# The experts of a second half's last token block are chosen once row 72 of the block ahead of it is with the vector engine

## The chip, the cores and the metric

The kernel runs on one core of a Trainium2 chip. The metric is device time in microseconds (us) from launch to end. Five engines work side by side: TensorE (PE in the profile, its weight loads PEld), VectorE (DVE), ScalarE (ACT), GpSimd (POOL) and SyncE (SP). Each takes its instructions in the order in which they stand in its own list. SP does nothing here but start plain DMAs; POOL does little but start the gathers, which are DMAs whose source rows come from a list of indices.

## The reference, cut to what matters

Two layers of a decoder over 512 tokens of width 1024. A layer mixes tokens in three ways (a gated recurrence, attention, a state-space scan), projects, adds, and ends with a layer of experts:

```python
for l in range(2):
    u = rms_norm(x, ...) @ w_in[l]
    m = concat([hgrn2(u), dilated_attention(u), ssd(u)])
    h = x + m @ w_out[l]
    x = h + peer(rms_norm(h))
# peer, for each token: 8 heads; a head scores 2 x 128 sub-keys, keeps the best 16 of either
# half, and of their 256 sums the best 16: an expert is (i, j), one of 128 x 128
# gate = softmax over the 16; down, up: tables of 16384 rows of 1024
# y = sum over the 8 x 16 = 128 chosen experts of  up[e] * gate[e] * gelu(<down[e], h_norm>)
```

For each token 128 rows of `down` and 128 rows of `up` are wanted, at places that depend on the data.

## The kernel before

**Tiling.** The 512 tokens are four blocks of 128. A half h is two blocks, j = 0 and 1. So (l, h, j) names a block of a layer. A *row* is one of a block's 128 experts for all its 128 tokens: one gather of 128 x 1024 float32 (512 KB), and one VectorE instruction that uses it.

**The pieces.** The mixers of a half are m00, m01, m10, m11 (layer, half). `choose` picks the experts of a half in four groups, (j, g) = (0,0), (0,1), (1,0), (1,1): g is which four heads. A group is about a hundred short VectorE instructions with a few of ScalarE between them. It ends with a write of 64 columns of the block's index list, `idx`. With four groups in each of four halves there are sixteen choices, numbered here 0 to 15 in order: 4 to 7 are layer 0's second half, 12 to 15 layer 1's. `experts_down` (d010 is layer 0, half 1, block 0) gathers rows of `down`: rows 0 to 63 use the indices of group g = 0, rows 64 to 127 those of g = 1; VectorE then multiplies the row by the normed tokens and sums (`g<-g,xn`), into column i of `a`. `experts_up_rows` (u010, u011, u111) gathers rows of `up`, and VectorE adds them to the block (`xv<-g,c,xv`). `experts_up_dense` (u00 for the first half of layer 0, u10 for layer 1's and the third block) does the same sum without gathers: SP streams the whole table as 128-row tiles `u`, VectorE builds one-hot operands (`oj`, `oi`, `co`) from the indices, PE turns them into coefficients `ct` (the builds: `ps<-co,oj`) and multiplies `u` by these (the uses: `ps<-u,ct`). At its end VectorE adds PE's sums to the tokens (`ux<-ux,ps`).

**What sets the order.** Three queues of Python generators are interleaved by a virtual clock: fg (m00, m01, u00, m10, m11, u10), bg (all experts_down and experts_up_rows) and tk (choose). A generator that yields "?x" waits until another has yielded "x". `experts_down` yields "?t.." ahead of row 64, `choose` of a second half yields "?b.." ahead of its second group (the first build of the dense part has been written down). The stream is then put in the engines' lists by a list scheduler that works with its own estimate of times; `behind(a, b)` tells it that `a` has to come after `b` on their engine, without a semaphore. Here every first `max` of choices 5, 6, 7 (and 13, 14, 15) stands behind `lead[l][-1]`, the last `co` of the first build, and rows 0 to 31 of d010 and d110 behind the others of `lead[l]`, two rows to one `co`. Buffers: eight for gathered rows, seven for weights and `u` tiles.

**How the pieces meet.** u00 runs beside d010 and d011; its end (`ux`) lets m10 begin, beside which u010 and u011 run. m11 needs u011 and the tokens of the second half, and after it come layer 1's d110 and d111 beside u10, and u111. On VectorE all are in one list. The profile puts nearly all instructions on L1383, the line of the helper that records them; the gathers are on L1068.

Of the kernel before, what the change touches and what calls it, by code (L numbers as in the profile page):

```python
# [29 lines left out]
FIRST = 0  # L30
AHEAD = 2
BIAS_AT = 16
ROWS = ((0, 1), (1,))
PE_ROWS = ((0, 0), (0, 0))
D = 1024
# [80 lines left out]
def hybrid_kernel(ctx: ExitStack, tc: tile.TileContext, x, w, small, rows, keys_t, rel_bias,  # L116
# [23 lines left out]
    def scr(shape, tag, dt=F32, bufs=None, pool=None):  # L140
        cnt[0] += 1
        return (pool or scope[0]).tile(shape, dt, name=f"{tag}_{cnt[0]}", tag=tag, bufs=bufs or BUFS.get(tag))

    def keep(shape, tag, dt=F32, bufs=4):
        return scr(shape, tag, dt, bufs=bufs, pool=pp)
# [83 lines left out]
    lead = [[] for _ in range(L)]  # L229
# [730 lines left out]
    def choose(l, h):  # L960

        e = st[l, h]
        qp = e.pop("qp")
        scr = lambda shape, tag, dt=F32, bufs=2: keep(shape, "k" + tag, dt, bufs)
        for j, g in ((0, 0), (0, 1), (1, 0), (1, 1)):
            if h and (j, g) == (0, 1):
                yield f"?b{l}"
            if (j, g) == (0, 1):
                yield f"?m{l}{h}"
            if g == 0:  # L970
# [11 lines left out]
            for c in range(2):  # L982
                sb = scr([P, 4, P], "s2")
                S.activation(sb, pc[c], AF.Copy, scale=e["y"][j])
                for a in range(4):
                    o, oi, i = sv[:, c, a, :], si[:, c, a, :], sb[:, a, :]
                    r = V.max(o[:, 0:8], i)
                    if h and (j or g):
                        behind(r.ins, lead[l][-1])
                    elif not h and (j or g):  # L990
                        behind(r.ins, e["last"])
                    V.max_index(oi[:, 0:8], o[:, 0:8], i)
                    V.match_replace(i, o[:, 0:8], i, -3e38)
                    V.max(o[:, 8:16], i)
                    V.max_index(oi[:, 8:16], o[:, 8:16], i)
                    yield
# [19 lines left out]
            r = scr([P, 2, 64], "rk")  # L1016
# [30 lines left out]
            r = V.tensor_tensor(e["idx"][j][:, 64 * g:64 * g + 64], ij[:, 0], ij[:, 1], OP.add)  # L1047
# [12 lines left out]
    def behind(ins, lead):  # L1060

        tc.add_manual_dep(ins, lead.name,
                          mybir.DependencyInfo(mybir.DependencyClass.NoSync, mybir.DependencyReason.DATA),
                          reason="the leading work first")

    def gather(table, idx, i):
        t = gslot([P, D])
        nc.gpsimd.indirect_dma_start(out=t, out_offset=None, in_=table,  # L1068
                                     in_offset=bass.IndirectOffsetOnAxis(ap=idx[:, i:i + 1], axis=0))
        return t  # L1070


    def experts_down(l, h, j):
        d = st[l, h]
        a = scr([P, P], "a", pool=pp, bufs=1)
        for i in range(P):
            if i == 64:
                yield f"?t{l}{h}{j}1"
            t = gather(down, d["idx"][j], i)
            r = V.scalar_tensor_tensor(t, t, 1.0, d["xn"][j], op0=OP.mult, op1=OP.mult, accum_out=a[:, i:i + 1])  # L1080
            g = i // RPG
            if (h, j) == (1, 0) and g < len(lead[l]):
                behind(r.ins, lead[l][g])
            yield
        u = scr([P, P], "u", pool=pp, bufs=1)
        c = keep([P, P], "c")
        V.tensor_tensor(u, a, a, OP.mult)
        V.tensor_scalar(u, u, 0.044715, 1.0, op0=OP.mult, op1=OP.add)
        V.tensor_tensor(u, u, a, OP.mult)
        V.tensor_scalar(u, u, -2.0 * math.sqrt(2.0 / math.pi), 80.0, op0=OP.mult, op1=OP.min)  # L1090
        S.activation(u, u, AF.Exp)
        V.tensor_tensor(a, a, d["gate"][j].rearrange("p a b -> p (a b)"), OP.mult)
        V.tensor_scalar(u, u, 1.0, None, op0=OP.add)
        V.reciprocal(u, u)
        V.tensor_tensor(c, a, u, OP.mult)
        d.setdefault("c", []).append(c)
        yield
# [4 lines left out]
    def experts_up_rows(l, j, n_pe):  # L1102

        d = st[l, 1]
        xv = keep([P, D], "xv", bufs=1)
        nc.sync.dma_start(xv, xd[(2 + j) * P:(3 + j) * P, :])
        on_pe = [i for i in range(P) if spread(i, n_pe)]
        acc = [bank([P, 512]) for _ in range(2)] if on_pe else []
        for i in range(P):
            t = gather(up, d["idx"][j], i)  # L1110
            if i in on_pe:
                dg = keep([P, P], "dg", bufs=2)
                S.activation(dg, ident, AF.Copy, scale=d["c"][j][:, i:i + 1])
                for n in range(2):
                    PE.matmul(acc[n], dg, t[:, n * 512:(n + 1) * 512], start=(i == on_pe[0]), stop=(i == on_pe[-1]))
            else:
                V.scalar_tensor_tensor(xv, t, d["c"][j][:, i:i + 1], xv, op0=OP.mult, op1=OP.add)
            yield
        for n, p in enumerate(acc):
            o = xv[:, n * 512:(n + 1) * 512]  # L1120
            V.tensor_tensor(o, o, p, OP.add)
        nc.sync.dma_start(out_rows(l, 2 + j), xv)
        yield
# [161 lines left out]
    def first():  # L1285
        def later():
            for _ in range(BIAS_AT):
                yield
            yield from make_bias()
# [10 lines left out]
    for l in range(L):  # L1300
        for h in range(2):
            tk.append((f"k{l}{h}", lambda l=l, h=h: choose(l, h), [f"p{l}{h}"]))
            for j in range(2):
                bg.append((f"d{l}{h}{j}", lambda l=l, h=h, j=j: experts_down(l, h, j), [f"t{l}{h}{j}0"]))
        for j in ROWS[l]:
            bg.append((f"u{l}1{j}", lambda l=l, j=j: experts_up_rows(l, j, PE_ROWS[l][j]), []))
# [5 lines left out]
    while any(pos[k] < len(queues[k]) for k in range(NQ)):  # L1312
        ready = []
        for k in range(NQ):
            if pos[k] == len(queues[k]):
                continue
            if gen[k] is None:
                name, f, deps = queues[k][pos[k]]
# [29 lines left out]
        if k == 1:  # L1348
            f = fg[pos[0]][0] if pos[0] < len(fg) else ""
# [115 lines left out]
```

## Time and profile before

| | us |
|---|---|
| runs | 3186.52, 3188.92, 3195.61 |
| median | 3188.92 |
| the profiled execution, its own time | 3198.11 |
| its span | 3196.2 |
| busy: PE, VectorE, POOL, ScalarE | 2409.3, 2680.0, 1778.9, 645.2 |

The span is from the first to the last instruction, and 1.9 us of the execution lie outside it. Times below are us from the span's start. VectorE is the busiest engine (84%), DMA stands near its full share in most of the forty slices, and PE is full where the dense part runs. No one of them fills the span: which one holds it up changes from stage to stage, so it is read stage by stage.

### The profile page before, as it was taken

The numbers are of one execution on the slowest core, as the hardware profiler recorded it, in microseconds if no ns is written. First come the engines' busy times: TensorE is split into PE (matmuls) and PEld (weight loads), VectorE is DVE, ScalarE is ACT, GpSimd is POOL, SyncE is SP. The second block draws the span as 40 slices with busy tenths as digits, with TensorE's granted clock in tenths as the row PEclk, the third lists the DMA queues.
The fourth block names the chain that finished last, engine by engine and source line by source line (L and its number), as shares of the span: only waits on it lengthen the run. The fifth ranks groups of instructions, "written<-read, shape, count | busy, mean of one in ns | idle before, by whom it ended". The sixth has DMA issues, their size and how long they took to land.

```text
span 3196.2 us, 45630 instructions
## 1 busy us (share of the span) xinstructions
PE 2409.3 (75%) x16115; PEld 1485.9 (46%) x16115; DVE 2680.0 (84%) x6050; ACT 645.2 (20%) x2076; POOL 1778.9 (56%) x1425
## 2 busy tenths in 40 slices
PE   7888777512999999687760467773189999799878
PEld 6776554411555554465540345543145455444423
DVE  7669998799999886587889999978999988878852
ACT  4554331100110000234220144221111110101100
POOL 0006677477346565475657666775752665666530
PEclk9889876755999999898585688676589999899999
DMA  5439999988769999999899999898785999899998
GB/s 189 143 109 339 356 337 329 335 292 303 289 262 397 358 359 415 350 399 358 295 373 369 403 346 366 304 355 317 260 329 180 395 371 362 298 402 357 377 420 332
DMA packets 291745, 1049.27 MB, mean 328 GB/s; under 512 B 33040, under 2 KB 33936, under 8 KB 291516
## 3 DMA queue, kind: packets, MB, share of 16 engines
q0 software_dynamic: 203824, 740.27, 62.1%
q1 hardware_dynamic: 87692, 306.08, 25.5%
q8 instruction: 127, 2.08, 0.2%
q14 instruction: 102, 0.84, 0.1%
HBM read 1037.82 MB, written 10.37 MB: 328 GB/s over the span
## 4 chain that ended last, share of the span: by engine, by line
PE 34%; DVE 32%; issue 13%; DMA 12%; POOL 5%; ACT 3%; POOLq 0%; DVEq 0%; SPq 0%; ACTq 0%
PE ps L1383 34%; DVE g L1383 14%; DMA g<-in_down_dram,idx 7%; POOL g L1068 5%; DMA g<-in_up_dram,idx 5%; DVE ksi L1383 2%; DVE oj L1383 2%; DVE xv L1383 2%; DVE co L1383 2%; DVE ks L1383 2%; DVE keq L1383 2%; DVE ksv L1383 1%; ACT s L1383 1%; DVE s L1383 1%; DVE krk L1383 1%
## 5 line engine op out<-in xcount | busy, mean ns | idle before, releaser
L1068 POOL DMA_INDIRECT g<-in_down_dram,idx x1024 | 1323.4, 1292 | 849.9 <-DVE g L1383 281.0
L1383 DVE SCALAR_TENSOR_TENSOR g<-g,xn 128x1024 f32<-128x1024 f32 x1024 | 1226.5, 1218 | 120.8 <-DMA g<-in_down_dram,idx 118.5
L1383 PE MATMUL ps<-u,ct 128*128 128x512 f32 x2560 | 1157.1, 604 | 34.4 <-DMA u<-in_up_dram 33.6
L1383 PEld LDWEIGHTS ps<-u,ct 128*128 128x128 f32 x2560 | 475.5, 192 | 616.9 <-issue 531.7
L1068 POOL DMA_INDIRECT g<-in_up_dram,idx x384 | 447.4, 1165 | 286.2 <-DVE xv L1383 172.1
L1383 DVE SCALAR_TENSOR_TENSOR xv<-g,c,xv 128x1024 f32<-128x1024 f32 x384 | 492.2, 1282 | 97.3 <-DMA g<-in_up_dram,idx 84.1
L1383 PE MATMUL ps<-co,oj 128*128 128x32 bf16 (+1 forms) x7296 | 214.0, 180 | 238.1 <-DVE co L1383 237.1
L1383 PEld LDWEIGHTS <-oj 128*128 128x128 bf16 x7296 | 209.2, 98 | 308.8 <-DVE co L1383 173.5
L1383 ACT ACTIVATE ct<-ps 128x128 f32<-128x128 f32 (+1 forms) x704 | 128.7, 278 | 933.3 <-PE ps L1383 933.2
L1383 PE MATMUL ps<-ident,s 128*128 128x128 f32 (+1 forms) x276 | 67.7, 388 | 281.3 <-ACT s L1383 240.1
L1383 DVE TENSOR_TENSOR oj<-ijt,iota_j 128x2048 bf16<-128x2048 bf16 x152 | 184.2, 1216 | 58.4 <-PE ps L1383 58.4
L1383 PEld LDWEIGHTS ps<-ident,s 128*128 128x128 f32 (+1 forms) x276 | 45.4, 197 | 297.6 <-ACT s L1383 248.9
L1383 DVE TENSOR_TENSOR co<-oi,cp 128x768 bf16<-128x768 bf16 (+1 forms) x304 | 161.7, 569 | 12.3 <-PE ps L1383 12.2
L1383 ACT ACTIVATE s<-ps 128x512 f32<-128x512 f32 (+5 forms) x143 | 62.3, 439 | 166.4 <-PE ps L1383 151.4
L752 POOL MEMSET diag<- 128x256 f32 x4 | 1.3, 316 | 162.3 <-DVE ksv L1383 162.3
L1383 PE MATMUL ps<-g,g 128*128 128x256 f32 (+2 forms) x280 | 89.7, 321 | 1.5 <-DVE g L1383 1.5
L1383 PE MATMUL ps<-T,g 128*128 128x256 f32 x400 | 81.7, 301 | 3.1 <-ACT T L1383 3.1
L1383 DVE DVE_READ_ACCUMULATOR g<-g,xn 128x1 f32 x1024 | 80.6, 79 | 0.0
L1383 DVE MAX8 ksv<-ks 128x8 f32<-128x128 f32 x256 | 57.4, 277 | 22.5 <-ACT ks L1383 22.5
L1383 DVE TENSOR_TENSOR oi<-ijt,iota_j 128x512 bf16<-128x512 bf16 x160 | 65.6, 415 | 6.1 <-ACT ijt L1383 6.1
L1383 PEld LDWEIGHTS ps<-T,g 128*128 128x128 f32 x400 | 67.7, 204 | 5.0 <-ACT T L1383 3.8
L1383 DVE FIND_INDEX8 ksi<-ksv,ks 128x8 uint16<-128x128 f32 x256 | 68.9, 282 | 0.0
(389 smaller groups left out, 2867.1 us busy)
## 6 DMA issues: line engine op xcount, KB each, us to landing
u<-in_up_dram SPq DMA_DIRECT2D x352, 512.0 KB, 6.9
g<-in_down_dram,idx POOLq DMA_INDIRECT x1024, 7.2
g<-in_up_dram,idx POOLq DMA_INDIRECT x384, 8.2
w00out<-in_w_dram SPq DMA_DIRECT2D x8, 512.0 KB
w00q<-in_w_dram SPq DMA_DIRECT2D x8, 512.0 KB
xd<-s SPq DMA_DIRECT2D x8, 512.0 KB, 2.6
w01out<-in_w_dram SPq DMA_DIRECT2D x8, 512.0 KB, 6.8
w01q<-in_w_dram SPq DMA_DIRECT2D x8, 512.0 KB, 7.4
```

Of the source, the lines that this page charges most:

```text
L752: G.memset(diag, 0.0)
L1068: nc.gpsimd.indirect_dma_start(out=t, out_offset=None, in_=table, in_offset=bass.IndirectOffsetOnAxis(ap=idx[:, i:i + 1], axis=0))
L1383: r = f(*a, **k)
```

## The change

Three edits. In `choose` of a second half, group (1,0) isn't begun until the mark "i{l}" has been given. `experts_down` of (l, 1, 0) gives this mark after row 72 has been written down, and keeps that row's VectorE instruction as `mid`. And the first `max` of the groups of block j = 1 stand behind that instruction, where they stood behind the last `co` of the first build; group (0,1) stays behind that `co`. No instruction is added or taken away. First halves are as they were.

```diff
+
+MID = 72
 ...
         for j, g in ((0, 0), (0, 1), (1, 0), (1, 1)):
             if h and (j, g) == (0, 1):
                 yield f"?b{l}"
+            if h and (j, g) == (1, 0):
+                yield f"?i{l}"
 ...
                     r = V.max(o[:, 0:8], i)
                     if h and (j or g):
-                        behind(r.ins, lead[l][-1])
+                        behind(r.ins, e["mid"] if j else lead[l][-1])
 ...
             if (h, j) == (1, 0) and g < len(lead[l]):
                 behind(r.ins, lead[l][g])
+            if (h, j, i) == (1, 0, MID):
+                d["mid"] = r.ins
+                yield f"i{l}"
             yield
```

What this does to the engines' lists is seen best on VectorE. First where choice 5 ends, which gives d010 the indices of its rows 64 to 127. In these rows `idx_5173` is that list; `krk`, `kpi`, `kpf`, `kts`, `gate`, `kss` with other numbers than 6676 and 6698 are choices 6 and 7; `oj`, `oi`, `co` are builds; `g..,a_5561` is a row of d010. Before:

```order
L1383 TENSOR_REDUCE kss_7399<-gate_6781 128x4
L1383 SCALAR_TENSOR_TENSOR krk_6958<-kpf_6956,krk_6958 128x64
L1383 CAST kpi_6957<-krk_6958 128x64
L1383 TENSOR_TENSOR krk_6676<-keq_6698 128x64
L1383 RECIPROCAL kss_7399<-kss_7399 128x4
L1383 SCALAR_TENSOR_TENSOR krk_6958<-kpf_6956,krk_6958 128x64
L1383 TENSOR_TENSOR oj_8022<-ijt_5935,iota_j 128x2048
L1383 TENSOR_TENSOR kpi_6957<-sixteen,kpi_6957 128x64
L1383 TENSOR_TENSOR co_8026<-oi_7937,cp_5936 128x768
L1383 TENSOR_TENSOR idx_5173<-krk_6676 128x64
```

and in the changed kernel, where the line numbers are seven higher:

```order
L1390 TENSOR_TENSOR keq_6698<-keq_6698 128x4x32
L1390 TENSOR_TENSOR krk_6676<-keq_6698 128x64
L1390 TENSOR_TENSOR idx_5173<-krk_6676 128x64
L1390 TENSOR_TENSOR oj_7489<-ijt_5935,iota_j 128x2048
L1390 TENSOR_TENSOR co_7493<-oi_7404,cp_5936 128x768 x2
L1390 TENSOR_TENSOR oi_7578<-ijt_5935,iota_j 128x512
L1390 SCALAR_TENSOR_TENSOR g_7496,a_5561<-g_7496,xn_904_5084 128x1024
L1390 SCALAR_TENSOR_TENSOR g_7505,a_5561<-g_7505,xn_904_5084 128x1024
L1390 TENSOR_TENSOR oj_7576<-ijt_5935,iota_j 128x2048
```

The list of choice 5 is written before choices 6 and 7 have begun, and row 64 follows four instructions of the builds later. Choice 6 now begins at row 78 of d010 and choice 7 at row 87 (both stood ahead of row 64); in layer 1 the two begin at rows 92 and 102.

Next, on VectorE too, from the end of d010 to d011, whose rows are `g..,a_8898` before and `g..,a_8904` now (`c_...` is the last instruction of d010's block). Before, the list of choice 6 had long been written, at row 79:

```order
L1383 TENSOR_SCALAR u_8828<-u_8828 128x128
L1383 RECIPROCAL u_8828<-u_8828 128x128
L1383 TENSOR_TENSOR c_8829<-a_5561,u_8828 128x128
L1383 SCALAR_TENSOR_TENSOR g_8899,a_8898<-g_8899,xn_909_5103 128x1024
L1383 SCALAR_TENSOR_TENSOR g_8908,a_8898<-g_8908,xn_909_5103 128x1024
```

Now it is `idx_7660`, and stands behind all 128 rows of d010:

```order
L1390 TENSOR_TENSOR c_8835<-a_5561,u_8834 128x128
L1390 TENSOR_TENSOR krk_7867<-keq_7889 128x64
L1390 SCALAR_TENSOR_TENSOR krk_8147<-kpf_8145,krk_8147 128x64
L1390 TENSOR_TENSOR kpi_8146<-sixteen,kpi_8146 128x64
L1390 TENSOR_TENSOR idx_7660<-krk_7867 128x64
L1390 SCALAR_TENSOR_TENSOR krk_8147<-kpf_8145,krk_8147 128x64
```

Thirteen rows of the list follow, none a gathered row, and then row 0 of d011; choice 7's list is written at row 13 of d011. Layer 1 has the same at d110 and d111.

The third place, on VectorE again, is the end of u00 (`ux`), in d011's second half. Before, with `g_10685` as row 107 of d011:

```order
L1383 SCALAR_TENSOR_TENSOR g_10675,a_8898<-g_10675,xn_909_5103 128x1024
L1383 SCALAR_TENSOR_TENSOR g_10685,a_8898<-g_10685,xn_909_5103 128x1024
L1383 TENSOR_TENSOR ux_11487<-ux_11487,ps_6455 128x512
L1383 SCALAR_TENSOR_TENSOR g_10688,a_8898<-g_10688,xn_909_5103 128x1024
L1383 TENSOR_TENSOR ux_11487<-ux_11487,ps_6456 128x512
```

and now, with `g_10859` as row 117:

```order
L1390 SCALAR_TENSOR_TENSOR g_10849,a_8904<-g_10849,xn_909_5103 128x1024
L1390 SCALAR_TENSOR_TENSOR g_10859,a_8904<-g_10859,xn_909_5103 128x1024
L1390 TENSOR_TENSOR ux_11481<-ux_11481,ps_6455 128x512
L1390 SCALAR_TENSOR_TENSOR g_10862,a_8904<-g_10862,xn_909_5103 128x1024
L1390 TENSOR_TENSOR ux_11481<-ux_11481,ps_6456 128x512
```

The barrier moved ten rows back in the list. In layer 1 the builds for the third block stand behind row 72 of d111 where they stood behind row 65, and the end of the first two blocks (`ux` of u10) behind row 53 of u111 where it stood behind row 47. On SP the write of u111's result, `out_dram<-xv`, is the 571st row where it was the 578th: seven fetches of `u` that stood ahead of it are now behind it.

## Rows read from the trace of the kernel before

**Rows 1.** Page, sections 1 and 2: busy us, then forty slices (tenths)

```profile
PE 2409.3 (75%) x16115; PEld 1485.9 (46%) x16115; DVE 2680.0 (84%) x6050; ACT 645.2 (20%) x2076; POOL 1778.9 (56%) x1425
DMA  5439999988769999999899999898785999899998
```

**Rows 2.** Windows, layer 0 and layer 1: busy by engine, clock, DMA share, GB/s

```profile
850.00:910.00 60.00, 59.48 (x546) 32.06 (x545) 60.00 (x316) 10.98 (x37) 0.00 (x0) 1.00 0.39 128
930.00:1050.00 120.00, 117.05 (x900) 60.29 (x899) 114.80 (x221) 12.61 (x61) 82.49 (x62) 0.99 1.01 398
1060.00:1195.00 135.00, 135.00 (x1071) 70.29 (x1068) 112.90 (x191) 13.36 (x68) 82.80 (x61) 1.00 0.97 359
1290.00:1310.00 20.00, 19.59 (x46) 8.36 (x44) 2.95 (x5) 0.33 (x2) 0.85 (x1) 1.00 0.60 204
1340.00:1571.00 231.00, 191.69 (x1166) 144.30 (x1164) 192.41 (x239) 79.02 (x243) 159.53 (x130) 0.82 0.97 369
1744.00:1766.00 22.00, 0.00 (x0) 0.00 (x0) 21.43 (x17) 0.00 (x0) 16.90 (x17) 0.50 1.02 410
2397.00:2463.00 66.00, 66.00 (x606) 35.54 (x605) 65.16 (x349) 12.60 (x48) 5.35 (x5) 1.00 0.41 138
3016.00:3137.00 121.00, 96.01 (x194) 33.00 (x195) 61.97 (x49) 0.00 (x0) 45.62 (x49) 1.00 1.03 420
3156.00:3192.00 36.00, 32.50 (x76) 13.87 (x74) 0.86 (x2) 0.00 (x0) 0.00 (x0) 1.00 0.77 292
```

**Rows 3.** Timelines at the hole of d010: start, duration, engine, instruction, [idle before]

```profile
857.11 1.22 DVE L1383 SCALAR_TENSOR_TENSOR g<-g,xn 128x1024 f32<-128x1024 f32 x1
916.39 1.31 POOL L1068 DMA_INDIRECT g<-in_down_dram,idx  x1 [73.63 <-DVE idx L1383]
921.95 1.23 DVE L1383 SCALAR_TENSOR_TENSOR g<-g,xn 128x1024 f32<-128x1024 f32 x1 [0.46 <-DMA g<-in_down_dram,idx]
```

**Rows 4.** Timeline of VectorE at the end of u00

```profile
1278.79 1.23 DVE L1383 SCALAR_TENSOR_TENSOR g<-g,xn 128x1024 f32<-128x1024 f32 x1 [0.83 <-DMA g<-in_down_dram,idx]
1307.05 0.69 DVE L1383 TENSOR_TENSOR ux<-ux,ps 128x512 f32<-128x512 f32 x1 [27.02 <-PE ps L1383]
```

**Rows 5.** PE at m11's start; tile xv on VectorE in 1740 to 1768 (min/median/max ns, first to last)

```profile
1805.08 1.97 PE L1383 MATMUL ps<-ident,s 128*128 128x128 f32 x8 [127.32 <-ACT s L1383]
L1383 DVE SCALAR_TENSOR_TENSOR xv<-g,c,xv x22: 1284/1285/1286, 1739.9 to 1767.6; 128x1024 f32<-128x1024 f32 x22
```

**Rows 6.** Timeline of VectorE between u010 and u011

```profile
1584.05 1.28 DVE L1383 SCALAR_TENSOR_TENSOR xv<-g,c,xv 128x1024 f32<-128x1024 f32 x1 [6.04 <-DMA xv<-xd]
```

**Rows 7.** Waits: total, times, longest; VectorE in 1060 to 1195, PE in 2340 to 2540

```profile
DVE oj L1383 <- PE ps L1383: 22.1, 15, 2.6
PE ps L1383 <- DVE co L1383: 5.1, 2, 2.8
```

**Rows 8.** PE's timeline where a build came late in layer 0

```profile
940.54 0.48 PE L1383 MATMUL ps<-co,oj 128*128 128x32 bf16 x11 [2.95 <-DVE co L1383]
```

**Rows 9.** Page, section 5: busy, mean ns, then idle before and its releaser

```profile
L1383 DVE MAX8 ksv<-ks 128x8 f32<-128x128 f32 x256 | 57.4, 277 | 22.5 <-ACT ks L1383 22.5
```

**Rows 10.** The end: VectorE's timeline, then the SP queue's

```profile
3154.10 1.28 DVE L1383 SCALAR_TENSOR_TENSOR xv<-g,c,xv 128x1024 f32<-128x1024 f32 x1 [1.16 <-DMA g<-in_up_dram,idx]
3190.97 0.69 DVE L1383 TENSOR_TENSOR ux<-ux,ps 128x512 f32<-128x512 f32 x1 [35.59 <-PE ps L1383]
3155.41 0.34 SPq L1122 DMA_DIRECT2D out_dram<-xv  x1
3155.85 24.28 SPq L1167 DMA_DIRECT2D u<-in_up_dram  x18
```

## The prediction

> **What bounds the kernel now.** I read the page's busy shares first, then its forty slices, then windows stage by stage, then single waits. VectorE is busy 84% of the span, PE 75%, and DMA stands at 9 tenths in most slices [rows 1], so no engine is the bound all through. The windows name it for each stage.
>
> *Choosing the experts of a second half.* From 850 to 910 VectorE is full (60.00 of 60 us), POOL starts no gather, and DMA falls to 0.39 of its time. Layer 1 has the same at 2397 to 2463, with 0.41 [rows 2]. Row 63 of d010 starts at 857.11 and row 64 at 921.95: a hole of 65 us in the rows, in which VectorE works on choices 5, 6, 7 and builds together, and POOL waits 73.63 us for the list of choice 5 [rows 3]. VectorE isn't idle there; what is lost is DMA time, some 0.6 of 65, or 39 us a layer.
>
> *The dense part u00.* PE is full from 1060 to 1290 and sets the end of the stage, while VectorE and DMA have room: VectorE is busy 112.90 of 135 us [rows 2], with 22.1 us spent in 15 waits of `oj` for PE [rows 7]. At 1278.79 VectorE has done row 107 of d011. Then it stands 27.02 us at `ux`, which waits for PE's last product [rows 4]; the eight gather buffers are full by then, so DMA falls to 0.60 in 1290 to 1310 [rows 2].
>
> *From there to m11.* PE has room now: it is idle 127.32 us before m11 begins at 1805.08 [rows 5], since m11 needs all rows of u010 and u011. These rows run at DMA 0.97 to 1.02 [rows 2]. At the end of u011 22 rows start in 27.7 us, 1.32 us a row [rows 5]. So whatever makes u011 end sooner moves m11 and all of layer 1 with it.
>
> *Layer 1's dense part* is again PE's, until at 3016 DMA becomes the bound (1.03, PE busy 96.01 of 121) [rows 2], and PE's last products end the kernel: VectorE waits 35.59 us for them [rows 10].
>
> **The change, part by part.** VectorE's work is the same, instruction for instruction. What moves is the order.
>
> 1. *The hole shrinks.* I added up, with durations from the trace, what VectorE has to do from row 40 of d010 to row 64: 115 us in the list of before, 74 in the new one, since most of choices 6 and 7 now stands behind row 64. So row 64 comes about 40 us sooner and the hole is near 24 us. Price by itself: nothing. VectorE was full in the hole, and up to row 0 of d011 the same sum gives 241 and 233 us. The gain exists only if rows now fill idle time of VectorE that was lost later.
>
> 2. *Ten rows come ahead of the `ux` barrier.* Row 107 stood ahead of it and now row 117 does, because rows have filled the 22.1 us [rows 7], and some of the 27.02 us [rows 4]. PE's end, and so the barrier's time, stays where it was. Ten rows of `down` fewer are left after it, and what is left, u010 and u011 with them, is a string that DMA and VectorE run without slack. At 1.32 us a row [rows 5] that is 13 us. Bounds: by the slowest stretch of that string, u010 beside m10, 231 us for 128 rows, or 1.8 us a row (the window 1340 to 1571) [rows 2], it is 18; if only six rows keep their lead, which is what stands in the list at the last normed tokens of m10, it is 8. I take 13, since the row that ends the string has the price 1.32. At u011's start VectorE sits 6.04 us behind a reload of `xv` [rows 6]; the lead can hide a part of that, and I count none.
>
> 3. *PE's gaps.* PE waited for late `co` twice in layer 1, 5.1 us together [rows 7], and once in layer 0, 2.95 us [rows 8]. In the new list the builds come 5 to 14 us of VectorE work sooner at these places, since two choices less stand ahead of them. Layer 0's gap moves the `ux` barrier, but the ten rows are counted against that barrier, so I take -1 from it. In layer 1 PE is the bound: between 0 and -5, I take -3, for the second gap lies behind d110's row 64, where the moved choices now stand.
>
> 4. *Layer 1's rows.* In d100 and d101 the lists are two rows later than before: +1. From d110 to u111 the lead is six rows at the end. There a row and a `u` tile share the DMA: 49 rows in 121 us, 2.47 us a row [rows 2]. u111 ends 6 x 2.47 = 15 us sooner than at 3154.10 [rows 10]. But SP meets its write of u111's result, and waits on it, seven tiles sooner in its queue, so 25 tiles stand behind the write, not 18 [rows 10]. Once the rows are over PE needs 32.50 us for 18 tiles, 1.8 us each [rows 2]: +12.6. Left: -2 (0 to -5).
>
> 5. *What the new order adds.* Choice 6 now ends only after row 127 of d010: between that row and row 0 of d011 lie 15 us of VectorE's work that is no row (21 in layer 1). `idx` is written some 4 us of work ahead of row 0, and from the list to the first row it took 5.6 us (916.39 to 921.95) [rows 3]: VectorE may sit 2 us here, once a layer. While VectorE is held by this, PE eats its store of coefficients. At row 64 PE had nothing left before [rows 8]; where the new list stands at its tightest I make PE's store 14 us in layer 0 and 20 in layer 1. So 2 to 10 us of idle VectorE cost PE nothing, but the rows come that much later: I count +1, from 0 to +4, and more than PE's store is a rival below.
>
> Sum: -13 - 3 - 1 + 1 - 2 + 1 = -17, taken against the profiled execution: 3198.1 - 17 = 3181. That execution is 9.2 us over the median of the three runs, so the median goes from 3188.9 to 3172. With every bound on its good side it is -18 - 5 - 3 + 1 - 5 + 0 = -30, and on its bad side -8 - 0 - 0 + 1 - 0 + 4 = -3.
>
> **A rule that speaks against it.** A gather's start took POOL 82.80/61 = 1.36 us beside builds (1060 to 1195), and 16.90/17 = 0.99 us where VectorE did nothing but rows (1744 to 1766) [rows 2]. Choices 6 and 7 had 31 rows beside them and now have 63, so 32 x 0.37 = 12 us of POOL time are added. POOL was busy 82.49 of 120 us where rows and choices met [rows 2], so I count none of it. The Trainium skill, SBUF — State Buffer, section "SBUF: two separate sides", says that GpSimd can't write the descriptors of its DMAs while a VectorE instruction in a two-port mode holds the port they share, so that transfers seem blocked by VectorE. The 1.36 beside 0.99 agree with it in sign. By that rule choices are best kept where no gather is started, which is where they stood; were all 12 us on the path, the sum would be -5.
>
> **The rivals.**
>
> *Given back (no difference).* DMA is at 0.97 over u010's stretch [rows 2]. If the ten rows ahead only change places with other transfers, if m10's steps come later by as much as the rows come sooner (VectorE's work in all is the same), or if the 12 us of POOL time turn out to lie on the path, u011 ends 0 to 5 us sooner. For it: VectorE is busy only 192 of 231 us beside u010, so m10's own chain sets part of the pace there. Against it: from 1744 nothing but rows runs, at full DMA, and a row done sooner is a row less. Then -2 to -9 in all: 3180 to 3187.
>
> *PE starves (slower).* One choice at a time is a chain between VectorE and ScalarE. Over all sixteen choices `ksv` waited 22.5 us for `ks` [rows 9], on average 1.4 us a choice; the scores are only the first of a choice's waits on ScalarE, and ScalarE now has the copies for PE's builds between them. If VectorE loses more than 14 us between row 40 of d010 and the tightest place, in the third of u00's four builds, PE stalls and the `ux` barrier moves. Say 30 us are lost in either layer: 30 - 14 = +16 there, against the -13, and 30 - 20 = +10 in layer 1, where the -3 goes as well: 16 - 13 + 10 + 1 - 2 = +12, so 3201. For it: PE's gaps before show that VectorE's builds are just in time [rows 7, 8]. Against it: 1.4 us a choice is far from 15, and builds and rows stand between the steps of the lone choices and can fill the waits.
>
> *The change does nothing.* If the scheduler had left the lists alone, the time would be 3189. The lists differ as shown, so I give it hardly a chance.
>
> **How the numbers follow.** The forecast, most of it between 3160 and 3182: 0.66. Given back: 0.22. PE starves: 0.10. Nothing: 0.02. A measurement of this kernel can tell about 0.3% from no change, 9.6 us here, so faster means under 3179.3. Of the forecast 0.62 lie there and 0.04 above, of the given-back case 0.01: faster 0.63, within 0.3% 0.27, slower 0.10. The range leaves out the starving case, a third of the given-back one and a little of the forecast's good side: 3159 to 3188.
>
> **What would show it.** Right: row 64 of d010 some 24 to 30 us after row 63, and DMA over 0.6 in the hole; `ux` at 1307 or a little sooner, with row 117 done ahead of it; VectorE's wait there near 15 us; m11's first product at about 1790 where it was 1805.08; PE's gaps for `co` in 2340 to 2540 under 5.1 us; the end 2 to 5 us nearer to m11 than before. Wrong: `ux` later than 1310 with PE waiting for `co` between 900 and 1100 (PE starves); m11's start within 5 us of before though row 117 is ahead of `ux` (given back); a wait of VectorE for gathers at d011's row 0 of much over 6 us (part 5).

## The result, and the profile after

On the chip of the first runs the changed kernel took 3167.61 us (four runs, 3165.54 to 3176.63) where the kernel before took 3189.77: a ratio of 0.9938, interval 0.9916 to 0.9960. A later set on another chip gave 0.9944 (0.9925 to 0.9963). On a third chip, which runs the kernel before at 3232 us, it gave 1.0005 (0.9979 to 1.0030). So the gain of 22 us is real on the chip it was forecast for and on one other, and isn't there on a third; both are taken up below.

The page of the changed kernel, busy shares and the slices of DMA, against [rows 1]:

```profile
PE 2399.5 (76%) x16115; PEld 1479.5 (47%) x16115; DVE 2680.9 (84%) x6050; ACT 645.8 (20%) x2076; POOL 1777.6 (56%) x1425
DMA  5439999888798999999899999898888979899998
```

VectorE's work is the same to 1 us. Windows of the changed kernel (columns as in [rows 2]), the first, second, third and fourth of them at the places of [rows 2], the last at the hole of layer 1:

```profile
850.00:910.00 60.00, 60.00 (x469) 31.30 (x468) 52.41 (x145) 7.63 (x35) 24.42 (x21) 1.00 0.67 255
930.00:1050.00 120.00, 116.84 (x922) 60.25 (x921) 117.75 (x364) 16.11 (x68) 58.63 (x43) 1.00 0.85 307
1060.00:1195.00 135.00, 131.95 (x1024) 68.13 (x1023) 120.32 (x207) 12.37 (x64) 88.91 (x66) 0.99 1.00 390
1290.00:1310.00 20.00, 20.00 (x48) 8.93 (x47) 0.04 (x1) 0.00 (x0) 0.00 (x0) 1.00 0.67 248
2380.00:2446.00 66.00, 66.00 (x528) 34.41 (x527) 57.50 (x152) 6.54 (x33) 31.95 (x26) 1.00 0.75 292
```

DMA in the hole rises from 0.39 to 0.67, and in layer 1 from 0.41 to 0.75. It falls from 1.01 to 0.85 in 930 to 1050, where the moved choices now are. And PE, which was full from 1060 to 1195, has lost 3 us there. The places of [rows 3] and [rows 4] in the timelines:

```profile
854.21 1.22 DVE L1390 SCALAR_TENSOR_TENSOR g<-g,xn 128x1024 f32<-128x1024 f32 x1
877.64 1.68 POOL L1072 DMA_INDIRECT g<-in_down_dram,idx  x1 [37.41 <-DVE idx L1390]
882.56 1.22 DVE L1390 SCALAR_TENSOR_TENSOR g<-g,xn 128x1024 f32<-128x1024 f32 x1 [2.65 <-DMA g<-in_down_dram,idx]
1283.31 1.23 DVE L1390 SCALAR_TENSOR_TENSOR g<-g,xn 128x1024 f32<-128x1024 f32 x1 [0.90 <-DMA g<-in_down_dram,idx]
1309.95 0.69 DVE L1390 TENSOR_TENSOR ux<-ux,ps 128x512 f32<-128x512 f32 x1 [25.41 <-PE ps L1390]
```

Row 64 starts 28.4 us after row 63, not 64.8. The row ahead of `ux` is now row 117. Counted from d010's row 0 it starts 7.3 us later than row 107 did, and `ux` comes 5.6 us later itself, so the wait there is still 25.41 us.

These four executions differ by up to 10 us ahead of d010, where nothing was changed (d010's row 0 starts at 734.8 and 732.0 in the first two traces, at 725.1 and 728.9 in the later pair). So stages are compared from that row on. Worked out from the starts and ends of rows and products in the traces, us:

| | before | changed | before, 2nd chip | changed, 2nd chip |
|---|---|---|---|---|
| d010 row 63 to row 64 | 64.8 | 28.4 | 65.1 | 30.2 |
| u00's products: their length | 516.0 | 521.3 | 514.8 | 520.7 |
| end of u00's last product, from d010's row 0 | 574.8 | 580.4 | 573.8 | 580.9 |
| d100's row 0 (u011 has ended), from d010's row 0 | 1051.2 | 1042.8 | 1050.1 | 1043.1 |
| d100's row 0 to u10's first product (m11) | 547.3 | 541.2 | 549.6 | 541.6 |
| u10's products, first to last | 858.5 | 854.3 | 858.3 | 850.9 |
| d010's row 0 to the last product | 2457.0 | 2438.4 | 2458.0 | 2435.6 |

The two pairs agree in the main: 7 to 8 us come from layer 0, 6 to 8 from m11's stretch, 4 to 7 from layer 1's dense part.

### The profile page after: what moved, and what is told of

Read it like the earlier page. It is cut to its first block, busy times and chain, and to the rows that moved or that the text cites. A ratio compares the mean times of both kernels' runs of the same rounds, so it can differ in the third digit from the quotient of the medians.

```text
span 3174.9 us, 45599 instructions
## 1 busy us (share of the span) xinstructions
PE 2399.5 (76%) x16115; PEld 1479.5 (47%) x16115; DVE 2680.9 (84%) x6050; ACT 645.8 (20%) x2076; POOL 1777.6 (56%) x1425
## 4 chain that ended last, share of the span: by engine, by line
DVE 37%; PE 34%; DMA 11%; issue 10%; POOL 4%; ACT 3%; DVEq 0%; POOLq 0%; ACTq 0%
PE ps L1390 34%; DVE g L1390 17%; DMA g<-in_down_dram,idx 7%; POOL g L1072 4%; DMA u<-in_up_dram 4%; DVE oj L1390 3%; DVE co L1390 3%; DVE ksi L1390 2%; DVE ks L1390 2%; DVE ksv L1390 2%; DVE keq L1390 1%; ACT s L1390 1%; DVE xv L1390 1%; DVE krk L1390 1%; DVE oi L1390 1%
## 5 line engine op out<-in xcount | busy, mean ns | idle before, releaser
L1390 PE MATMUL ps<-u,ct 128*128 128x512 f32 x2560 | 1159.1, 605 | 30.9 <-DMA u<-in_up_dram 30.1
L1390 DVE TENSOR_TENSOR co<-oi,cp 128x768 bf16<-128x768 bf16 (+1 forms) x304 | 161.7, 568 | 10.8 <-PE ps L1390 10.8
L1390 DVE TENSOR_TENSOR ux<-ux,ps 128x512 f32<-128x512 f32 x10 | 6.6, 681 | 74.0 <-PE ps L1390 74.0
```

What stands on the lines that cost most here:

```text
L1390: r = f(*a, **k)
```

## The experiments

Ten kernels, two of them twice, were timed in four sets on four chips. The chips differ: they run the kernel before at 3223, 3232, 3189 and 3232 us. The first set had one layer's change at a time, and two tests of the explanation in the prediction.

**The change in one layer.** Layer 0 alone, then layer 1 alone (the edit for layer 0; layer 1's has 1 in the place of this 0):

```diff
-            if h and (j, g) == (1, 0):
+            if h and l == 0 and (j, g) == (1, 0):
                 yield f"?i{l}"
-                        behind(r.ins, e["mid"] if j else lead[l][-1])
+                        behind(r.ins, e["mid"] if j and l == 0 else lead[l][-1])
-            if (h, j, i) == (1, 0, MID):
+            if (l, h, j, i) == (0, 1, 0, MID):
```

> The change in layer 0 alone (mark, wait and `mid` only for l = 0). Theory 'rows ahead of the barrier', with the sizes read from the trace of the changed kernel: u011's end 8 to 11 us sooner, and 5 us more at the end of m11, where two rows less stand ahead of the tokens' sum; layer 1's dense part as before (858 us): ratio 0.9945 to 0.9965, 3172 to 3178. Rival 'both layers alike' (the hole costs the same in each): half of the 22 us, ratio 0.9965, with the dense part of layer 1 unchanged and nothing gained at the end of m11.

> The change in layer 1 alone. Theory 'rows ahead of the barrier': no barrier stands behind layer 1's hole but the end of the kernel, where rows and `u` tiles share the DMA, so only 3 to 5 us come off the dense part (858 to 854), all of them after the last row of u111: ratio 0.9985 to 0.999, 3184 to 3187. m11 starts at 1805 as before. Rival 'both layers alike': 10 us or more, ratio 0.9965.

Measured: 0.9998 (0.9971 to 1.0025) and 0.9999 (0.9968 to 1.0031). Neither theory has its number. This is the chip with 3223 us. In the trace of layer 0 alone u00's products took 551.6 us, not 521; what that is worth is taken up under the slower chips. Layer 1 alone has its dense part at 861.1 us; the three other traces of this set and the next one with layer 1's old order and no second edit there lie at 866.0, 866.2 and 868.4. That is the 4 to 7 us of the table, but on scattered values. The split by layer rests on the table, not on these two ratios.

**Only `ux` held back** (kernel before, the additions of `ux` behind row 117 of d011; the mark "e0" is given once that row has been written down).

```diff
+            if l == 0 and n == len(plan) - 1:
+                yield "?e0"
             for b in blocks:
                 if uses[b][-1] == n:
 ...
-                        V.tensor_tensor(o, o, acc[b][e], OP.add)
+                        r = V.tensor_tensor(o, o, acc[b][e], OP.add)
+                        if l == 0:
+                            behind(r.ins, st[0, 1]["hold"])
```

> The kernel before, with one thing moved: in layer 0 the four `ux` additions may not be taken by VectorE before row 117 of d011 (before: row 107). The choices stay where they were, so the 65 us hole in d010 stays. In the list ten rows more are then done when m10 ends (row 165 of the two `up` blocks against 155). Theory 'rows ahead of the barrier': the gain in layer 0 is made by those rows alone, since the 27 us wait takes them in; u011 ends 10 x 1.32 = 13 us sooner, and a part of the 6 us reload of `xv` is hidden, so 3170 to 3176 (ratio 0.994 to 0.996), with `ux` still at 1307 +- 2 and a wait of some 10 us there. Rival 'the hole': DMA time lost in the hole is what costs, rows 108 to 117 aren't there in time, `ux` comes 10 us or more late, and the time is 3187 to 3195 (ratio 0.999 to 1.002).

Measured: 1.0111 (1.0066 to 1.0156). The edit was too narrow to test anything. On VectorE the first to wait for PE was now m10's `hS`, in front of the ten rows, and on POOL the gathers stood behind m10's `diag`:

```profile
1307.46 0.27 DVE L1390 MEMSET hS<- 128x256 f32 x1 [23.61 <-PE ps L1390]
1307.47 0.31 POOL L752 MEMSET diag<- 128x256 f32 x1 [24.91 <-issue]
1318.96 2.48 DVE L1390 TENSOR_TENSOR ux<-ux,ps 128x512 f32<-128x512 f32 x4
```

So the rows still came after PE's end, and `ux` 11.7 us after it, where in the kernel before its first addition starts 2.5 us ahead of that end (1307.05 and 1309.59). A barrier is every instruction that waits for the same event, on every queue.

**Two buffers for the block of `experts_up_rows`** (kernel before, `bufs=1` to `bufs=2` in the tile `xv`).

> The kernel before, with two buffers for the block that `experts_up_rows` adds to, where there was one: u011's load doesn't have to wait for u010's store. It tests the 6.04 us that VectorE stood at that load, and what is behind it, m10's `mix`. If it lies on m10's path (as the changed kernel's trace suggests: m10 ran 3.8 us late up to there and 2.9 us early after it), m11 starts 4 to 8 us sooner: ratio 0.9975 to 0.999. In the list eight rows more are done when m10 ends (163 against 155), and five fewer at the end of m11; if rows left are what counts, another 8 x 1.32 = 10 us come off, ratio 0.994 to 0.996. If the load wasn't on the path: 0.999 to 1.001.

Measured: 0.9972 (0.9941 to 1.0003). u011 starts 2.4 us after u010's last row started, where in the kernel before it was 13.1, and d100's row 0 comes 1056.4 us after d010's row 0; layer 1 alone, which has the kernel before's order in this stretch and ran in the same set, has 1062.1. But of these 5.7 us 2.6 are there at the end of u00 already (578.7 and 581.3), where the two kernels are alike. So 3 us at most are left for the reload, in one trace of either, and the ratio doesn't separate it from no change: that it lies on m10's path is not shown.

**The whole barrier held back.** Now `ux`, m10's VectorE instructions and POOL's `diag` are behind row 117 (for `diag`: the gather of row 125), in the kernel before; and behind row 126 (`diag`: row 127), in the changed kernel, without and with the second buffer. `held` is set in u00's end and in m10:

```diff
+                yield "?e0"
+                meter.hold, meter.behind, meter.held = st[0, 1]["row"], behind, True
 ...
-            G.memset(diag, 0.0)
+            r = G.memset(diag, 0.0)
+            if (l, h) == (1, 0):
+                behind(r.ins, st["gm"])
 ...
+                    if kind == "dve" and meter.held:
+                        meter.behind(r.ins, meter.hold)
```

> The changed kernel itself, beside the kernels of this set and on their chip, since the chip of the earlier set runs the kernel before at 3223 us where the first chip ran it at 3190, and both one-layer versions stood at 1.000 there. If the gain belongs to the order of the instructions, the ratio is 0.992 to 0.996 here too. If it belongs to the first chip's faster DMA (on a slower chip PE waits for `u` tiles that the earlier rows push aside, as the profile of the version for layer 0 alone shows between 1208 and 1260), it is 0.998 to 1.003.

> The kernel before with the whole barrier between u00 and m10 moved behind row 117 of d011: the `ux` additions, m10's first VectorE instructions (which wait for PE's last product as well) and, on POOL, the `diag` memset behind the gather of row 125. Choices and hole stay as they were; PE's list is the same up to there. Theory 'rows ahead of the barrier': the wait of 27 us takes the ten rows in, PE ends u00 when it did before, `ux` comes within 2 us of that, m10 ends when it did and 10 rows less are left (165 against 155): 8 to 13 us, and up to 5 at m11's end (714 against 716): ratio 0.994 to 0.997. Rival 'the hole': without the time won in the hole the ten rows come late, `ux` slips by 5 us or more: 0.999 to 1.003.

> The changed kernel with the same barrier moved on, from row 117 to row 126 of d011. At 117 VectorE still waits 25.4 us, and nine rows at 2.0 us beside `u` tiles are 18. Theory 'rows ahead of the barrier': nine rows less after m10 (170 against 161), 9 x 1.32 = 12 us less than the changed kernel, ratio to before 0.988 to 0.992 (0.996 of the changed kernel). Rival 'full': the DMA has no room for nine more rows before PE's end, and rows ahead take tiles from PE: the same as the changed kernel or up to 6 us more.

> As the one before it, with two buffers for the block that u010 and u011 add to. On its own that edit gave 0.997 (0.994 to 1.000). Theory: with the barrier at row 126 the reload has long been done when m10's last `mix` comes, so the load itself is worth nothing; but rows 170 to 176 are also ahead when m10 ends, 6 x 1.32 = 8 us: 0.9855 to 0.990. Rival: the two edits hide the same 6 us, and it equals the one before it.

Measured on one of the slower chips: 1.0005 (0.9979 to 1.0030), 1.0019 (0.9992 to 1.0045), 1.0016 (0.9984 to 1.0047) and 0.9989 (0.9966 to 1.0012). The last two don't beat the changed kernel clearly, and are no better version. What the set shows is that the changed kernel's gain isn't there on this chip, so the decisive kernels were run again:

> The kernel before, unchanged, to have its trace from the chip of this set. If the chip is like the first: 3186 to 3196 us, SP's queue never waits for what the profile calls remote, u00's products end at 1308 to 1313. If it is like the two slower ones: 3215 to 3240 us. Theory 'rows push SP's transfers aside' then expects that the kernel before is spared in u00 (its products end at 1307 to 1320, as in the four traces that have this order there) and that `u` tiles aren't held for 38 us as they were in two of the three traces with the changed order. Rival 'the chip just stalls': a stall of 30 us or more in u00 here too.

> The changed kernel on the same chip. Like the first chip: ratio 0.992 to 0.996, 3163 to 3178 us. Like the slower ones: 0.998 to 1.003, and by the theory 'rows push SP's transfers aside' u00's products end 20 to 35 us later than in the kernel before of this set; by the rival both have it or neither.

> The kernel before with the whole barrier between u00 and m10 behind row 117 of d011, choices and hole as they were, once more. On a slower chip it gave 1.002 (0.999 to 1.005): there the ten rows were in time (d011 ended 21 us before where the kernel's one ends after `ux`), but SP's load of m10's weights then stood 50 us where it stands 25 elsewhere. On a chip like the first the theory 'rows ahead of the barrier' expects 0.994 to 0.997 and m11's start 8 to 13 us earlier; if it is 0.999 or more there as well, the rows ahead of the barrier aren't what gains, and the hole is.

This chip was like the first. Measured: 0.9999 (0.9986 to 1.0012), 0.9944 (0.9925 to 0.9963) and 1.0000 (0.9987 to 1.0014). So the ten rows put ahead of the barrier by hand gain nothing that the ratio shows, where the theory "rows ahead of the barrier" expected 0.994 to 0.997: it failed its own test, with a kernel that has costs of its own. The trace says where the rows went. It is of an execution of 3180.04 us, where the median is 3189.99, so it tells the places better than the sizes. The rows do come in time, and `ux` waits only 6.42 us:

```profile
1297.56 0.69 DVE L1396 TENSOR_TENSOR ux<-ux,ps 128x512 f32<-128x512 f32 x1 [6.42 <-PE ps L1396]
```

But u00's products end 577.7 us after d010's row 0, 3 to 4 later than in the kernel before, and m10's first product comes 10.5 us later. Of that 4.6 us are the edit's own: SP's queue now holds the store of the first block until both are added, and the first load of m10's tokens is issued 10.8 us after the first addition of `ux` started, not 6.2 (1308.38 against 1297.56; in the kernel before, in the same set, 1302.48 against 1296.29). d100's row 0 comes 2.5 us sooner, the stretch from there to u10's first product takes 542.3 us (so 5 to 7 less), and layer 1's dense part 861.4 (3 more): 6.6 us in this trace in all, which the median doesn't have. Row 117 was done 568.8 us after d010's row 0; in the changed kernel it was at 552.5. These 16 us are what the shorter hole gave. So neither the hole nor the rows ahead of the barrier were had by themselves: this kernel suggests that the lead without the hole's 16 us isn't enough, and none has the short hole without the lead on a chip like the first.

**The mark after row 100.**

```diff
-MID = 72
+MID = 100
```

> The change with the mark after row 100 in place of 72. The hole in d010 shrinks as much (choices 6 and 7 begin behind row 100), but the order differs in what the two theories count. Rows ahead of `ux` in d011: 112 (before 108, changed 118). Rows of u010 and u011 done when m10 ends: 158 (155, 161). Rows of d100 and d101 ahead of m11's last steps: 710 of the count in which before has 716 and the changed kernel 714. Rows of u111 ahead of layer 1's `ux`: 302 (303, 309). Theory 'rows left, and rows ahead of the mixer's steps': u011's end only 3 x 1.32 = 4 us sooner than before, the stretch from d100's row 0 to u10's first product 541 or less (before 547 to 550, changed 541 to 542), since six rows less stand ahead, and layer 1's dense part as before (858, not 851 to 854): ratio 0.995 to 0.998 on a chip like the first, 2 to 5 us slower than the changed kernel. Rival 'the hole': as much gained as by the changed kernel in both dense parts, ratio 0.993 to 0.995. On a slower chip the stretches alone are compared.

Measured: 1.0024 (1.0002 to 1.0046), on a slower chip: no gain, and if anything a little slower. m11's stretch was 560.0 us and the dense part 873.5. On the slower chips that stretch runs from 548 to 565 with all orders, so the expectation of 541 or less wasn't met, but can't be told apart either. That six rows less ahead of m11's steps gain more than two is not shown.

## The slower chips

Three traces from slower chips have the changed order of layer 0 with the barrier where that leaves it (the changed kernel, layer 0 alone, row 100). In all three u00's products take 548 to 555 us, where the other chips need 521. In the four traces from those chips with layer 0's old order they take 517 to 523. But the profiled execution of each of the three took 14 to 25 us more than its kernel's median (3250.72 against 3236.84, 3247.78 against 3228.43, 3266.89 against 3241.69), and was the longest of twelve. So they show what such an execution loses, and not what the median one does.

In the changed kernel's trace PE stands still in small pieces between products of `u` from 1216 on; the profile names nothing that it waits for. SP's queue waits as well, and the profile puts its wait down to no engine or DMA of this core ("remote"). The waits of SP's queue (what it waited for: us, times, longest), in 1190 to 1290 of the changed kernel, then in 1150 to 1300 of the one with row 100:

```profile
SPq L1174 <- remote: 51.2, 6, 38.6
SPq L1174 <- PE ps L1390: 41.7, 14, 4.3
```

```profile
SPq L1174 <- PE ps L1390: 89.8, 28, 4.4
SPq L1174 <- remote: 44.6, 3, 41.7
```

SP issues no `u` tile for some 40 us (38.7 to 41.8 from one issue to the next in the three traces; from 850 on, no other has more than 13.4 in u00). The DMA queues in 1212 to 1248 (packets, MB, share of the engines; q0 is what POOL starts, q1 what SP starts) of the changed kernel on the slower chip, then on the first chip:

```profile
q0 software_dynamic: 3928, 14.31, 98.2%
q1 hardware_dynamic: 151, 0.54, 4.0%
```

```profile
q0 software_dynamic: 2512, 9.15, 62.1%
q1 hardware_dynamic: 1624, 5.93, 40.3%
```

The DMA engines are full in both. On the slower chip the last tiles that SP issued land up to 1220, and from 1220 to 1240 its queue moves nothing. So from there on it isn't the gathers that push SP's tiles out of the engines: SP stands still, and the gathers take what it leaves.

In the five traces from the first chip and the one like it no wait of SP is put down to "remote"; all nine from the slower chips have such waits, 41 to 95 us in the four with layer 0's old order and 113 to 182 in the five with the changed one. But these sums are no loss. All these waits are on one semaphore (a counter that one engine raises and another waits for; number 110 in the traces), which only PE's instructions raise. So SP waits for PE there, as it does elsewhere, and "remote" says only that the profile found no PE instruction that ended near the update. The records of the slower chips are also thinner: 32,886 to 34,464 semaphore updates a trace, where the five others have 39,062 to 39,075. The same wait has either name. For the load of m11's weights as m11 begins (1780 to 1803 of the changed kernel on the first chip, 1833 to 1869 on the slower one):

```profile
SPq L390 <- PE ps L1390: 19.5, 1, 19.5
```

```profile
SPq L390 <- remote: 31.7, 1, 31.7
```

It is 18.7 to 20.5 us in the five traces and 30.1 to 32.5 in the nine, whatever the order. So of these waits some 11 us here are the slower chips' own, and not the whole of what is put down to "remote".

What is left is this: on the slower chips the gain isn't there in the medians, and in three executions, each well over its median, SP waits some 40 us for PE to release a buffer while PE has gaps. Why PE's count comes so late, and why that was seen with this order alone, was not found; a trace is one execution, and no kernel was run to take that wait away. Nor does the order alone bring it into u00: the two kernels with the barrier at row 126 have the changed order up to there, ran on such a chip, and took 527 and 529 us. Why the median execution gains nothing there stays open.

## Why the prediction was right, and where its steps were off

The forecast was 3172, -17 us; the median is 3167.6, -22 us, and the two pairs of traces give -18.6 and -22.3 from d010's row 0 on. The way and the size were right. The terms were less so: one was half its size, two had the wrong sign, and they made up for each other, so that the sum came out this near is in part luck. And the gain was found on two chips, not on a third.

1. *The hole.* Forecast 24 to 30 us and DMA over 0.6; measured 28.4 and 30.2, and 0.67. Right. That this alone is worth nothing, and all of it is in what rows can do later, was not tested by itself. The kernel with the hole left in and the rows ordered ahead by hand stayed at 1.0000, which suggests that the lead needs the hole's time; whether the time needs the lead it can't say.

2. *Ten rows, -13.* The list had them ahead of `ux`, as forecast. The step that failed is "PE's end, and so the barrier's time, stays where it was": the barrier came 6 to 7 us later (574.8 to 580.4, 573.8 to 580.9), with `ux` at 1309.95, on the edge of the sign that I had given (1310). A lead of ten rows at 1.32 us counts only against a barrier that stands still: 13 - 6 = 7, and d100's row 0 came 8.4 and 7.0 us sooner, with m11's first product at 1793.83 (forecast 1790). The wait at `ux`, forecast near 15 us, stayed at 25.41. The rows took 8 us from VectorE's waits for PE ([rows 7]: 22.1 us in 15 waits), and the rest out of the later barrier. The same group of waits (us, times, longest) in 1060 to 1195 of the changed kernel:

```profile
DVE oj L1390 <- PE ps L1390: 14.2, 9, 2.6
```

   Behind the barrier m10 ran up to 6.7 us late in the first pair and up to 9.9 in the second. In both it won back some 3.6 us ahead of the reload of [rows 6], for a reason that I did not find, and 3.3 at it, since the rows' lead now covers it: the first row of u011 waits for nothing (1571.31, no idle time before it). I had counted none of that. So m10 ended level in the first pair and 2.6 us late in the second, with six rows less to do, 8 us: the lower bound that I gave was near the true value, by way of a barrier that I had held fixed.

3. *PE's gaps, -1 in layer 0.* Wrong in sign. PE's waits for `co` during u00 rose from 4.8 to 9.0 us, and from 4.5 to 9.5 on the second chip, and its products took 5 to 6 us longer. That is most of what the barrier came late. (The prediction had seen only one of the two waits in the 4.8, 2.95 us.) Its waits in 792.5 to 1313 of the changed kernel:

```profile
PE ps L1390 <- DVE co L1390: 9.0, 4, 3.0
```

   A new gap stands where choice 7 and the end of d010 push the builds back:

```profile
1073.72 0.46 PE L1390 MATMUL ps<-co,oj 128*128 128x32 bf16 x11 [3.05 <-DVE co L1390]
```

   This is the rival "PE starves" in small. Its threshold, 14 us of idle VectorE, was put too high: VectorE idled 11.0 us from 860 to 1060. In layer 1 the gaps were 3.8 us in all where they were 5.1 [rows 7], so -1, not -3.

4. *Layer 1's rows, +1 for m11.* Wrong in sign, and the largest miss. I priced two rows moved behind m11's last steps as two rows late. My reading after the runs: m11 is a chain, PE waits for it, and what stands in front of its steps on VectorE delays it; rows there come 2.45 us apart (2124.62 to 2127.07 in the changed kernel), each waiting for its gather. PE waits for the sum of the tokens, before and then changed, in the first pair:

```profile
2149.58 1.97 PE L1383 MATMUL ps<-ident,s 128*128 128x128 f32 x8 [5.18 <-DVE s L1383]
```

```profile
2131.50 1.09 PE L1390 MATMUL ps<-ident,s 128*128 128x128 f32 x8 [0.61 <-DVE s L1390]
```

   In the second pair the same waits fall by 1.4 us only (2100 to 2165, before and then changed; us, times, longest):

```profile
PE ps L1383 <- DVE s L1383: 5.6, 2, 3.3
```

```profile
PE ps L1390 <- DVE s L1390: 4.2, 2, 2.8
```

   There 6.7 of the 8.0 us are won ahead of the end of m11's last projection, which comes before the sum; in the first pair it is 2.4 of 6.1. m11's stretch was 5 to 8 us shorter in all three traces with two rows less ahead (541.2, 541.6, and 542.3 in the kernel with the barrier held) than in the two without (547.3, 549.6). But the kernel with the barrier held also ran on a slower chip, and has the longest stretch of all there, 564.6. The two rows were not put back by themselves. So the gain in m11's stretch is measured, and its cause stays open; two rows at the sum explain at most the first pair. The end was as worked out: SP issued its 25 tiles behind the write of u111's result, which came 17 us sooner after u10's first product (forecast 15), and the last `ux` waited 48.37 us:

```profile
3121.69 37.05 SPq L1174 DMA_DIRECT2D u<-in_up_dram  x25
3169.58 0.69 DVE L1390 TENSOR_TENSOR ux<-ux,ps 128x512 f32<-128x512 f32 x1 [48.37 <-PE ps L1390]
```

   Forecast for layer 1's dense part -5, measured -4.2 and -7.4.

5. *The two new seams, +1.* VectorE waited 3.4 us for gathers at d011's row 0 (990 to 1060), forecast 2. Near enough.

The 12 us of POOL time that the prediction left open did not come: a gather's start took POOL 58.63/43 = 1.36 us in 930 to 1050 and 88.91/66 = 1.35 in 1060 to 1195, where [rows 2] have 1.33 and 1.36, and POOL's busy time in all went from 1778.9 to 1777.6 us. So the rule of the Trainium skill on GpSimd's descriptors (SBUF — State Buffer, section "SBUF: two separate sides") cost next to nothing here that was not there before: more choices beside the gathers made them hardly longer.

Of the rivals, "given back" describes half of layer 0's gain. (Its range should read -4 to -9, so 3180 to 3185: without the -13 the terms add up to -4.) Something like "PE starves" is in those three executions on the other chips, but not for want of VectorE's builds: the waits there are SP's for PE, and PE's gaps beside them.

## What to carry to other kernels

A lead in one engine's list is worth its rows only if the barrier stays; price what the same move does to the engine that sets the barrier, in the same sum. In front of a chain that another engine waits for, a row of bulk work may cost the time between two rows there (2.45 us here), and not what its own instruction takes (1.22); the runs do not settle it. Where a gain is under 1%, time it on more than one chip: here 0.994 on two chips was 1.000 on a third. And before a trace is used to explain a median, see how far its own execution lies from that: here the three that showed a stall lay 14 to 25 us above it.

## What the runs showed of the hardware

Chips differ by 1.3% on the same program (3189 to 3232 us). On the slower ones the load of m11's weights waits 30.1 to 32.5 us for PE in nine traces, and 18.7 to 20.5 in the five of the others. While SP stood still on a slower chip, the gathers alone filled the DMA engines (102.5% in 1220 to 1240 of the changed kernel, 8.39 MB), so busy DMA engines did not show that the tiles of `u` were on their way.
